# A hybrid decoder step: the four quadrant sums of each stationary unit on GpSimd, two of them a product earlier

## The chip, the cores and the metric

The kernel runs on one core of one Trainium2 chip. A core has TensorE (PE in the profile; its weight loads are PEld), VectorE (DVE), ScalarE (ACT), GpSimd (POOL) and SyncE (SP), which here only starts transfers, and 16 DMA engines. The time is the device time of one execution in microseconds. The kernel before takes 2857.4 us, the median of three runs (2855.56 to 2859.32). What is compared is the median of the changed kernel's runs with that of the kernel before.

## The reference

One inference step of one decoder layer for a prompt of 2048 rows and for 8 sample requests of 4 rows each, with shared weights, d = 1024, everything in fp32. Cut to what matters:

```python
m, s_gla, s_ssm, conv_buf = mixer(rmsnorm(x, lw['ln_mix_pre']), ...)   # two recurrent head groups
h = x + rmsnorm(m, lw['ln_mix_post'])                                  # m ends in  mixed @ w_out
a = cross_attend(rmsnorm(h, lw['ln_xa_pre']), mk, mv, w_xq, w_xo)      # softmax over 256 memory rows, 4 heads
h = h + rmsnorm(a, lw['ln_xa_post'])
hf = rmsnorm(h, lw['ln_ffn_pre'])
f = (jax.nn.silu(hf @ lw['w_gate']) * (hf @ lw['w_up'])) @ lw['w_down']  # d_ff = 2816
h = h + rmsnorm(f, lw['ln_ffn_post'])
```

The outputs are both hidden states, the recurrent states, the convolution's last rows and the memory's keys and values. The change touches the second part of the kernel, from `w_out` to `w_down`, which in the profiled execution begins at about 862 us and lasts to the end.

## The kernel before, in words

The first part makes the mixer's projections and its recurrence, chunk by chunk. The second part is a chain of nine passes over the prompt: `o` (`w_out`), `s` (attention scores), `v` (attention values), three blocks `g` of gate and up (over row groups 0 to 2, 3 to 5, and 6 to 7 with 16 sample columns beside them), and three parts `d` of the down projection. All of them are matrix products in fp32 that TensorE makes from pairs: each operand x is split into a rounded high part and a remainder, x = hi + lo, and a product is three matmuls, hi·hi, hi·lo and lo·hi (`three`, L134 to L136).

**Units and products.** Each pass multiplies many stationary *units* by seven moving *pieces*. A unit is a 2x2 arrangement of quadrants q0 to q3, and a block product is made from seven products in place of eight (a Strassen-Winograd scheme), taken in the order `TURN = [0, 1, 3, 2, 5, 4, 6]`. Three of the seven use q0, q1 and q3 themselves. The other four use sums of quadrants: S1 = q2 + q3 (product 3), S2 = S1 - q0 (product 2), S4 = q1 - S2 (product 5), S3 = q0 - q2 (product 4). S2 needs S1, and S4 needs S2. There are 114 units: 8 in each of `o`, `s`, `v`, 22 in each block `g` (11 column groups, gate then up) and 8 in each part `d`. So there are 456 sums, each 128 partitions by 512 columns (384 in the 8 units of the first part `d`).

**How one unit is prepared.** The class `Unit` (L1545 to L1578) loads the raw unit into a tile `raw` (two buffers, a transfer started by SyncE). `op` (L1554 to L1558) makes one sum into a tile `sum`, which has two buffers, so that the third and fourth sum of a unit reuse those of the first and second. `hi(i)` makes what product i needs: the sum, if there is one, then the high part into a tile `s` (four buffers) with a ScalarE copy (L1576), and it returns the VectorE instruction that makes the remainder (L1578), which is issued one product later. `part(e)` asks for this four products ahead of the product that TensorE is on (`ahead_ = 4`); it first issues the remainder of the entry before, then calls `hi` for its own.

**The moving side.** The class `Pieces` (L1609 to L1670) does the same for the pieces: ScalarE L1645 for the high part, VectorE L1649 for the remainder, from a staging tile `st` into tiles `r` (and `e`). This work is heavy where a pass begins. In the first and last unit of a pass it stands between the unit's own steps.

**Evacuation.** A unit's products go to three accumulators in PSUM (`accA`, two buffers, `accB` and `accC`, one each). `quads` (L1740) takes them out in `o`, `s` and `v` (ScalarE L1752, VectorE L1754), `evac_gate` (L1870) and `evac_up` (L1885) in the blocks `g`. There VectorE adds (L1902), multiplies by the gate (L1903) and in the third block the sample columns too (L1905), and a GpSimd transfer writes the result (L1909). `evac_d` does it for the parts `d`.

**What sets the order.** The order of each engine is the order in which the program issues: `pin` ties every instruction to the one issued before it on its engine. Per product the program issues the matmuls, the evacuation, `part` for the entry four ahead, a step of the moving side, then a step of the work that runs behind (`posts`, `aux`, `back`). An engine does not pass over an instruction that waits.

**GpSimd** has in this part the transfers to DRAM (`hX`, `out_y`, `xq`, `pT`, `xp`, `wT`, `aT`, `yp`), the one-column reciprocal roots of the norms (L142), and in the first block `g` some work of the samples (L1142).

Of the kernel before, what the change touches and what calls it, by code (L numbers as in the profile page):

```python
# [16 lines left out]
ALU = mybir.AluOpType  # L17
# [20 lines left out]
def f(ap):  # L38
    return ap.bitcast(F32)
# [3 lines left out]
def hymba_kernel(ctx: ExitStack, tc: tile.TileContext, a: dict, o: dict, dbg: dict | None = None):  # L43
    nc = tc.nc
# [75 lines left out]
    def wload(src, pieces=1, pool=None, raws=None):  # L120
        raw = (raws or wp).tile([P, 1024], F32, name="wraw", bufs=2)
        nc.sync.dma_start(out=raw, in_=src)
        hi, lo = ((pool or wp).tile([P, 1024], F32R, name=n, bufs=1 if pool else 3) for n in ("whi", "wlo"))
        w = 1024 // pieces
        with tc.high_priority(offset=AHEAD):
            for c in range(pieces):
                cs = slice(c * w, (c + 1) * w)
                last[0] = nc.scalar.activation(hi[:, cs], raw[:, cs], AF.Copy)  # L128
                nc.vector.tensor_tensor(lo[:, cs], raw[:, cs], f(hi)[:, cs], op=ALU.subtract)  # L129
        return raw, hi, lo  # L130
# [1414 lines left out]
    class Unit:  # L1545
# [8 lines left out]
        def op(self, out, x, y, o):  # L1554
            t, q = self.t, self.q
            t[out] = pf.tile([P, 512], F32, name="sum", bufs=2)[:, 0:self.w].rearrange("p (k c) -> p k c", c=P)
            x, y = (q[i] if isinstance(i, int) else t[i] for i in (x, y))
            nc.vector.tensor_tensor(t[out], x, y, op=o)  # L1558

        def hi(self, i):  # L1560

            if i == 1:
                self.op("S1", 2, 3, ALU.add)
            if i == 3:
                self.op("S2", "S1", 0, ALU.subtract)
            if i == 2:
                self.op("S4", 1, "S2", ALU.subtract)
            if i == 5:
                self.op("S3", 0, 2, ALU.subtract)
            v = {0: self.q[0], 1: self.q[1], 6: self.q[3]}  # L1570
            v = v[i] if i in v else self.t[{3: "S1", 2: "S2", 5: "S4", 4: "S3"}[i]]
            w = self.w
            s = pf.tile([P, 1024], F32R, name="s", bufs=4)
            hi, lo = s[:, 0:w], s[:, 512:512 + w]
            h3, l3 = (x.rearrange("p (k c) -> p k c", c=P) for x in (hi, lo))
            nc.scalar.activation(h3, v, AF.Copy)  # L1576
            self.got[i] = hi, lo
            return lambda: nc.vector.tensor_tensor(l3, v, f(h3), op=ALU.subtract)  # L1578
# [735 lines left out]
```

## Time and profile before

| | |
|---|---|
| median of the runs | 2857.4 us (2855.56, 2857.4, 2859.32) |
| the profiled execution's own time | 2854.98 us |
| its span | 2853.3 us |
| mean granted TensorE clock | 0.99 |
| TensorE, matmuls (PE) | busy 2757.0 us, 97% of the span |
| TensorE, weight loads (PEld) | 2362.4 us, beside the matmuls |
| VectorE (DVE) | 2074.9 us, 73%, 3820 instructions |
| ScalarE (ACT) | 1486.6 us, 52%, 2926 instructions |
| GpSimd (POOL) | 526.2 us, 18%, 716 instructions |
| the sums (L1558 on VectorE) | 228 + 114 + 114 instructions, median 0.68 to 0.69 us each |
| the remainders (L1578 on VectorE) | 456 from sums, 342 from raw quadrants, mean 0.68 us |
| the high parts (L1576 on ScalarE) | 456 from sums, 342 from raw quadrants, mean 0.62 us |

Busy time counts the running of instructions, not their waits, and starting a transfer is not busy time. A row of instructions in the profile reads: line, engine, operation, tile written, tiles read, shapes. Then come the count, the busy time with the mean of one in ns, and the idle time of the engine ahead of these instructions with what ended it. A row of the timeline reads: start in us, duration in us, engine, line, operation, and in brackets the idle time ahead and what ended it.

### The profile page before, as it was taken

Reading aid. Unit: us, or ns where it says so; the run is one execution under the profiler, and the core shown is the slowest. Engines: PE = TensorE matmul, PEld = TensorE weight load, DVE = VectorE, ACT = ScalarE, POOL = GpSimd, SP = SyncE. Lnnn points to the kernel's source line nnn. Section 1 sums busy time; section 2 is a strip of 40 time slices with the busy share of each in tenths; the row PEclk is TensorE's granted clock in tenths of the full one; section 3 lists DMA queues with packets and bytes.
Section 4 is the critical chain, followed back from the end, with each engine's and each line's share of the span. In section 5 each row is a group of like instructions: output and inputs, shape, how many; then the busy total and the mean of one; then the engine's idle time right before and its main releaser. Section 6 shows DMA issues by size and latency. Waiting matters only on the chain. (4 is left out here: it accounts for less than half of the span.)

```text
span 2853.3 us, 41834 instructions
## 1 busy us (share of the span) xinstructions
PE 2757.0 (97%) x15207; PEld 2362.4 (83%) x15207; DVE 2074.9 (73%) x3820; ACT 1486.6 (52%) x2926; POOL 526.2 (18%) x716
## 2 busy tenths in 40 slices
PE   8999999999997999999899999999999999999998
PEld 8887887787875878878798888889999998778786
DVE  7677777766747787677787787768678888564676
ACT  5545554544545777777754534434445555353432
POOL 2132342331321321015321110001000000000011
PEclk9999999999999999999999999999999999999999
DMA  7345535342256886468855566774234436574865
GB/s 252 115 135 181 153 106 163 111 146 88 79 180 227 295 278 223 148 188 254 275 200 187 186 222 233 263 251 165 97 130 176 150 122 208 185 213 102 244 150 131
DMA packets 151871, 514.27 MB, mean 180 GB/s; under 512 B 18336, under 2 KB 29776, under 8 KB 138096
## 3 DMA queue, kind: packets, MB, share of 16 engines
q1 hardware_dynamic: 95712, 336.01, 36.0%
q0 software_dynamic: 43712, 150.60, 16.6%
q10 hardware_dynamic: 12240, 24.99, 2.7%
q8 instruction: 120, 1.97, 0.3%
q14 instruction: 87, 0.71, 0.1%
HBM read 365.76 MB, written 145.76 MB: 179 GB/s over the span
## 5 line engine op out<-in xcount | busy, mean ns | idle before, releaser
L134 PE MATMUL accA<-r,s 128*128 128x512 f32 (+2 forms) x1792 | 641.8, 358 | 27.4 <-ACT r L1645 7.9
L136 PE MATMUL accA<-r,s 128*128 128x512 f32 (+2 forms) x1792 | 631.1, 352 | 1.7 <-DVE s L1578 1.6
L135 PE MATMUL accA<-r,s 128*128 128x384 f32 (+2 forms) x1472 | 504.8, 343 | 1.9 <-DVE r L1649 1.9
L134 PEld LDWEIGHTS accA<-r,s 128*128 128x128 f32 x1792 | 340.6, 190 | 86.3 <-issue 17.7
L1576 ACT ACTIVATE s<-sum 128x512 fp32r<-128x512 f32 (+1 forms) x456 | 282.3, 620 | 217.1 <-DVE sum L1558 92.1
L136 PEld LDWEIGHTS accA<-r,s 128*128 128x128 f32 x1792 | 340.2, 190 | 34.2 <-DVE s L1578 2.8
L134 PE MATMUL accC<-r,s 128*128 128x512 f32 (+2 forms) x896 | 318.6, 356 | 9.2 <-ACT s L1576 3.8
L1578 DVE TENSOR_TENSOR s<-sum,s 128x512 fp32r<-128x512 f32 (+1 forms) x456 | 305.6, 677 | 21.6 <-ACT s L1576 21.2
L136 PE MATMUL accC<-r,s 128*128 128x512 f32 (+2 forms) x896 | 314.2, 351 | 0.2
L135 PEld LDWEIGHTS accA<-r,s 128*128 128x128 f32 x1472 | 280.2, 190 | 21.3 <-DVE r L1649 5.0
L1578 DVE TENSOR_TENSOR s<-raw,s 128x512 fp32r<-128x512 f32 (+1 forms) x342 | 232.3, 679 | 52.5 <-ACT s L1576 50.7
L1576 ACT ACTIVATE s<-raw 128x512 fp32r<-128x512 f32 (+1 forms) x342 | 213.3, 624 | 72.0 <-PE accC L136 53.8
L135 PE MATMUL accC<-r,s 128*128 128x384 f32 (+2 forms) x736 | 250.5, 340 | 0.3 <-DVE r L1649 0.3
L128 ACT ACTIVATE whi<-wraw 128x1024 fp32r<-128x1024 f32 (+2 forms) x148 | 137.1, 940 | 187.6 <-PE acc L135 98.1
L129 DVE TENSOR_TENSOR wlo<-wraw,whi 128x1024 fp32r<-128x1024 f32 (+2 forms) x148 | 167.2, 1139 | 64.0 <-ACT whi L128 63.3
L134 PEld LDWEIGHTS accC<-r,s 128*128 128x128 f32 x896 | 168.9, 189 | 37.4 <-ACT sg L1877 5.3
L136 PEld LDWEIGHTS accC<-r,s 128*128 128x128 f32 x896 | 169.1, 189 | 16.2 <-DVE s L1578 0.9
L142 POOL TENSOR_TENSOR rs<-ms,nhalf 128x1 f32<-128x1 f32 (+4 forms) x125 | 113.4, 908 | 373.5 <-DVE ms L140 357.3
L134 PE MATMUL acc<-xh,whi 128*128 128x512 f32 (+1 forms) x464 | 168.5, 364 | 8.4 <-ACT xh L289 8.3
L136 PE MATMUL acc<-xh,wlo 128*128 128x512 f32 (+1 forms) x464 | 164.5, 356 | 1.7 <-DVE wlo L129 1.7
L135 PE MATMUL acc<-xl,whi 128*128 128x512 f32 (+1 forms) x464 | 164.1, 355 | 0.2 <-DVE xl L290 0.2
L134 PE MATMUL accB<-r,s 128*128 128x512 f32 (+2 forms) x448 | 157.6, 352 | 0.0
(644 smaller groups left out, 5847.9 us busy)
## 6 DMA issues: line engine op xcount, KB each, us to landing
raw<-in_w_gu_dram SPq DMA_DIRECT2D x66, 1024.0 KB, 4.9
wraw<-in_w_in_fm_dram SPq DMA_DIRECT2D x52, 512.0 KB, 3.7
wraw<-in_w_in_tm_dram SPq DMA_DIRECT2D x48, 512.0 KB, 3.7
st<-in_w_down_dram SPq DMA_DIRECT2D x37, 512.0 KB, 6.5
aT<-og POOLq DMA_DIRECT2D x22, 768.0 KB, 4.2
yp<-y POOLq DMA_DIRECT2D x32, 512.0 KB, 6.7
raw<-aT SPq DMA_DIRECT2D x16, 1024.0 KB, 6.4
out_y_dram<-y POOLq DMA_DIRECT2D x28, 512.0 KB, 6.0
```

What stands on the lines that cost most here:

```text
L128: last[0] = nc.scalar.activation(hi[:, cs], raw[:, cs], AF.Copy)
L129: nc.vector.tensor_tensor(lo[:, cs], raw[:, cs], f(hi)[:, cs], op=ALU.subtract)
L134: nc.tensor.matmul(ps, lhsT=wh, rhs=ah, start=start, stop=False, skip_group_check=more)
L135: nc.tensor.matmul(ps, lhsT=wh, rhs=al, start=False, stop=False, skip_group_check=more)
L136: nc.tensor.matmul(ps, lhsT=wl, rhs=ah, start=False, stop=stop, skip_group_check=more)
L142: nc.gpsimd.tensor_tensor(out=rs[:rows, :cols], in0=ms[:rows, :cols], in1=nhalf[:rows, :cols], op=ALU.pow)
L1576: nc.scalar.activation(h3, v, AF.Copy)
L1578: return lambda: nc.vector.tensor_tensor(l3, v, f(h3), op=ALU.subtract)
```

## The change

The four sums are made by GpSimd instead of VectorE. S1 is asked for together with product 0 of the unit instead of product 1, and S2 together with product 1 instead of product 3, each one entry of `TURN` earlier. S4 (with product 2) and S3 (with product 5) keep their places. What is computed, the tiles and their numbers of buffers are the same.

```diff
@@ -1555,13 +1555,13 @@
             t, q = self.t, self.q
             t[out] = pf.tile([P, 512], F32, name="sum", bufs=2)[:, 0:self.w].rearrange("p (k c) -> p k c", c=P)
             x, y = (q[i] if isinstance(i, int) else t[i] for i in (x, y))
-            nc.vector.tensor_tensor(t[out], x, y, op=o)
+            nc.gpsimd.tensor_tensor(out=t[out], in0=x, in1=y, op=o)
 
         def hi(self, i):
 
+            if i == 0:
+                self.op("S1", 2, 3, ALU.add)
             if i == 1:
-                self.op("S1", 2, 3, ALU.add)
-            if i == 3:
                 self.op("S2", "S1", 0, ALU.subtract)
             if i == 2:
                 self.op("S4", 1, "S2", ALU.subtract)
```

VectorE in the third block `g` (256 rows and 16 sample columns), around the evacuation of an up unit; `s` is the pair of a unit's operand, `sum` a sum, `t` and `og` the evacuation's tiles. Before:

```order
L1903 TENSOR_TENSOR og<-t,sg 128x2x128
L1905 TENSOR_TENSOR s_f<-t,sg 128x16
L1578 TENSOR_TENSOR s<-raw,s 128x512
L1558 TENSOR_TENSOR sum<-raw 128x512
L1902 TENSOR_TENSOR t<-accA,t 128x272
L1903 TENSOR_TENSOR og<-t,sg 128x2x128
L1905 TENSOR_TENSOR s_f<-t,sg 128x16
L1578 TENSOR_TENSOR s<-raw,s 128x512
L1558 TENSOR_TENSOR sum<-sum,raw 128x512
L1578 TENSOR_TENSOR s<-sum,s 128x512
L1558 TENSOR_TENSOR sum<-raw,sum 128x512
L1903 TENSOR_TENSOR og<-accA,sg 128x2x128
```

and now:

```order
L1903 TENSOR_TENSOR og<-t,sg 128x2x128
L1905 TENSOR_TENSOR s_f<-t,sg 128x16
L1578 TENSOR_TENSOR s<-raw,s 128x512
L1902 TENSOR_TENSOR t<-accA,t 128x272
L1903 TENSOR_TENSOR og<-t,sg 128x2x128
L1905 TENSOR_TENSOR s_f<-t,sg 128x16
L1578 TENSOR_TENSOR s<-raw,s 128x512
L1578 TENSOR_TENSOR s<-sum,s 128x512
L1903 TENSOR_TENSOR og<-accA,sg 128x2x128
```

The three sums are gone from VectorE's row; the rest stands in the order it had. Two remainders, which were apart by a sum, now follow each other.

GpSimd in the values pass `v`, where `y` is an evacuated row group, `u` and `st` what is written for the blocks `g`, and `rs` a reciprocal root. Before:

```order
L1852 DMA xp<-st 128x512 x2
L142 TENSOR_TENSOR rs<-ms,nhalf 128x1
L1725 DMA y<-hX 128x1024
L1852 DMA xp<-u 128x512 x2
L1796 DMA out_y_dram<-y 128x1024
L142 TENSOR_TENSOR rs<-ms,nhalf 128x1 x2
L1725 DMA y<-hX 128x1024
L1852 DMA xp<-u 128x512 x2
L1796 DMA out_y_dram<-y 128x1024
```

and now:

```order
L1852 DMA xp<-st 128x512 x2
L142 TENSOR_TENSOR rs<-ms,nhalf 128x1
L1725 DMA y<-hX 128x1024
L1852 DMA xp<-u 128x512 x2
L1558 TENSOR_TENSOR sum<-raw 128x512
L1796 DMA out_y_dram<-y 128x1024
L142 TENSOR_TENSOR rs<-ms,nhalf 128x1 x2
L1725 DMA y<-hX 128x1024
L1558 TENSOR_TENSOR sum<-sum,raw 128x512
L1852 DMA xp<-u 128x512 x2
L1558 TENSOR_TENSOR sum<-raw,sum 128x512
L1796 DMA out_y_dram<-y 128x1024
```

Three sums have come between GpSimd's transfers and roots: S1 ahead of the first output transfer, S2 and S4 around the two transfers of `xp`. The transfers and roots keep their order among themselves.

## The prediction

> **What bounds the kernel now.** I read the share of each engine first, then the engines' busy time in stretches cut at the points where a pass begins, then what TensorE waited for.
>
> ```profile
> PE 2757.0 (97%) x15207; PEld 2362.4 (83%) x15207; DVE 2074.9 (73%) x3820; ACT 1486.6 (52%) x2926; POOL 526.2 (18%) x716
> ...
> 862.00:912.00 50.00, 38.12 (x130) 26.26 (x131) 35.94 (x46) 29.07 (x47) 2.58 (x3) 0.88 0.59 207
> 1384.00:1420.00 36.00, 24.05 (x112) 20.69 (x111) 27.00 (x46) 25.46 (x55) 13.00 (x19) 0.85 0.83 274
> 1784.00:2134.00 350.00, 346.98 (x2091) 325.50 (x2090) 250.99 (x427) 157.26 (x294) 24.76 (x41) 1.00 0.52 181
> 2154.00:2384.00 230.00, 227.86 (x1768) 220.29 (x1768) 188.92 (x373) 123.96 (x253) 7.14 (x10) 1.00 0.42 147
> 2384.00:2398.00 14.00, 9.27 (x50) 7.58 (x49) 12.08 (x24) 6.17 (x12) 0.71 (x1) 0.76 0.73 251
> sum 1982.00, PE 1921.57 PEld 1670.00 DVE 1479.09 ACT 1060.73 POOL 279.09; mean PE 147.81 PEld 128.46 DVE 113.78 ACT 81.59 POOL 21.47
> ```
>
> The columns of a stretch are its length, then PE, PEld, DVE, ACT and POOL busy, the granted clock and the DMA load. The last row sums all stretches from 862 to 2844, where the units run. TensorE is busy 1921.6 of 1982.0 us, so it idles 60.4 us in all. Of that, 11.9 + 12.0 + 4.7 us lie in three short stretches in which a pass begins; inside a pass it idles 3.0 of 350 and 2.1 of 230 us. VectorE is busy 1479.1 (75%). Nothing that relieves VectorE can bring more than these 60.4 us and what the clock loses beside them. What ended TensorE's waits:
>
> ```profile
> PE accA L134 <- ACT r L1645: 7.9, 7, 3.8
> PE accA L135 <- DVE e L1649: 7.0, 8, 1.6
> PE accA L134 <- DVE y L1754: 5.8, 1, 5.8
> PE accA L134 <- DVE t L1902: 5.0, 2, 4.7
> ...
> PE accC L134 <- ACT s L1576: 3.8, 1, 3.8
> PE accA L134 <- ACT s L1576: 3.6, 2, 3.0
> ...
> PE accA L136 <- DVE s L1578: 1.6, 2, 1.3
> ```
>
> The pieces of the moving side (L1645, L1649) and two evacuations lead. The pairs that the four sums feed (s, L1576 and L1578) ended 9.0 us of waits in five places.
>
> **What it removes.** 456 sums leave VectorE; those of the block with most pressure are
>
> ```profile
> L1578 DVE TENSOR_TENSOR s<-sum,s 128x512 fp32r<-128x512 f32 x83 | 55.9, 684 | 4.2 <-ACT s L1576 4.2
> L1578 DVE TENSOR_TENSOR s<-raw,s 128x512 fp32r<-128x512 f32 x60 | 41.2, 686 | 4.6 <-ACT s L1576 3.8
> L1558 DVE TENSOR_TENSOR sum<-raw 128x512 f32<-128x512 f32 x41 | 28.2, 688 | 0.7
> L1558 DVE TENSOR_TENSOR sum<-raw,sum 128x512 f32<-128x512 f32 x21 | 14.5, 692 | 0.7
> L1558 DVE TENSOR_TENSOR sum<-sum,raw 128x512 f32<-128x512 f32 x21 | 14.4, 684 | 0.0
> L1903 DVE TENSOR_TENSOR og<-t,sg 128x256 f32<-128x256 f32 x31 | 13.2, 426 | 1.1
> ```
>
> which is VectorE from 2154 to 2384. At 0.69 us each, 456 sums are about 313 us, 21% of VectorE's work in the stage. By itself this is worth almost nothing, because the engine that waits is TensorE and it hardly waits for VectorE.
>
> **What it adds.** 456 two-operand sums on GpSimd. The trace has three like them, 128x512 in fp32:
>
> ```profile
> L778 POOL TENSOR_TENSOR xD<-xD,y x16: 1300/1592/1669, 153.4 to 785.6; 128x512 f32<-128x512 f32 x16
> L781 POOL TENSOR_TENSOR z<-xD,z x16: 1287/1296/1313, 158.8 to 789.0; 128x512 f32<-128x512 f32 x16
> L743 POOL TENSOR_TENSOR xw<-xdt,wl__6835 x4: 1038/1046/1047, 728.9 to 777.7; 128x512 f32<-128x512 f32 x4
> ```
>
> The three numbers are minimum, median and maximum in ns. L743 reads one operand as a broadcast of few columns; the sums read two dense ones like L781, so I take 1.30 us, with 1.04 and 1.67 as ends. 456 x 1.30 = 593 us on an engine that has 279 us in this stage: 872 of 1982 us, 44%. GpSimd has the room. The Trainium skill (GPSIMD Engine Reference, section 4.1, Engine selection) puts elementwise work on VectorE because GpSimd is about twice as slow with two inputs; 1.30 against 0.69 us is that ratio, so the trace agrees. Its 4497 ns for 2048 elements gives an estimate of 1.12 us, and 513 us for the 456.
>
> The price that counts is another. A GpSimd sum holds up a VectorE instruction that reads two operands from SBUF:
>
> ```profile
> 2202.70 1.28 DVE L1578 TENSOR_TENSOR s<-sum,s 128x512 fp32r<-128x512 f32 x2
> ...
> 370.90 2.36 DVE L765 TENSOR_TENSOR M<-M,cbm 128x512 f32<-128x512 f32 x2
> 371.06 1.65 POOL L778 TENSOR_TENSOR xD<-xD,y 128x512 f32<-128x512 f32 x1 [2.88 <-DVE y L777]
> ...
> 1547.39 1.03 POOL L1142 TENSOR_TENSOR Ms<-Ms,sell 128x512 f32<-128x512 f32 x1 [1.60 <-DMA Ms<-in_state_ssm_dram]
> 1547.46 1.51 DVE L1578 TENSOR_TENSOR s<-sum,s 128x512 fp32r<-128x512 f32 x1
> ```
>
> Two such instructions alone take 1.28 us; with one GpSimd instruction between them they take 2.36, so it costs VectorE 1.08 us. At 1547 the very instruction that follows our sums, the remainder L1578, takes 1.51 instead of 0.68 and ends 0.55 us after GpSimd does. The Trainium skill says why (Advanced Engine Details and Errata, GPSIMD Details): GpSimd shares a read and a write interface with VectorE and conflicts with two-SBUF-input instructions. These rows agree.
>
> So the sums do not leave that path; each takes 1.08 us (or up to 1.30, the whole instruction) of it instead of 0.64. In the tightest block, 2154 to 2384, the path carries 143 remainders at 0.64 (91.5), 13.2 of L1903 and 83 sums at 1.08 (89.6): 194 of 230 us, 84%; at 1.30 it is 213 us, 92%. It fits, barely. In the other blocks of gate and up the same work stands against a longer time: by 350 us for 22 units, where this one has some 21 in 230, it is below 65%.
>
> **What it moves.** S1 and S2 are asked for one product earlier. In the tightest block they stand in VectorE's densest run, and ScalarE waits for them:
>
> ```profile
> 2206.41 0.44 DVE L1902 TENSOR_TENSOR t<-accC,t 128x272 f32<-128x272 f32 x1 [1.45 <-PE accC L136]
> ...
> 2207.91 0.69 DVE L1558 TENSOR_TENSOR sum<-raw 128x512 f32<-128x512 f32 x1
> ...
> 2208.72 0.63 ACT L1576 ACTIVATE s<-sum 128x512 fp32r<-128x512 f32 x1 [1.75 <-DVE sum L1558]
> ...
> 2212.14 0.63 ACT L1576 ACTIVATE s<-sum 128x512 fp32r<-128x512 f32 x1 [0.71 <-DVE sum L1558]
> ...
> 2215.45 0.39 PE L134 MATMUL accC<-r,s 128*128 128x272 f32 x1
> ```
>
> With the new position S1 and S2 depend only on the raw tile and on buffers that are free by then, so they fall into the 1.45 us of rest before 2206.41 and the time before it. The third sum, S4, keeps its position; ScalarE splits it at 2212.14, after 0.71 us of waiting, and TensorE first uses it at 2215.45, 2.7 us after that split ends. Even 1.30 us plus one hold of 1.08 stays inside this. So: no stall from late sums, value 0, bounds 0 and the case below.
>
> S4 and S3 now also wait on GpSimd for remainders that VectorE makes of S1 and S2 (their two buffers are reused), and behind them stand GpSimd's own DMAs. The longest such delay is in the values pass:
>
> ```profile
> 1303.25 0.83 POOL L1796 DMA_DIRECT2D out_y_dram<-y  x1
> ...
> 1306.41 0.69 DVE L1578 TENSOR_TENSOR s<-sum,s 128x512 fp32r<-128x512 f32 x1 [0.17 <-ACT s L1576]
> ...
> 1316.46 0.59 ACT L1752 COPY y<-accC 128x512 f32<-128x512 f32 x1
> ...
> out_y_dram<-y POOLq DMA_DIRECT2D x28, 512.0 KB, 6.0
> ```
>
> S4 waits for the remainder that ends at 1307.10 and takes 1.30; the output DMA behind it goes at about 1308.4 instead of 1303.25, lands 6.0 us later at 1314.4, and the copy that reuses its buffer runs at 1316.46. Hidden, with 2 us to spare. Elsewhere a DMA or a reciprocal root behind one sum is late by one sum, 1.3 us, against a product of 2.0 us (twelve matmuls; 2091 of them in 350 us), 1.6 in the tightest block (1768 in 230).
>
> **The sum.** (1) The first unit: S1 and S2 leave a dense run of VectorE for the rest that stands ahead of it.
>
> ```profile
> 863.25 1.23 DVE L1649 TENSOR_TENSOR r<-st,r 128x1024 fp32r<-128x1024 f32 x1 [2.95 <-ACT r L1645]
> ...
> 866.46 0.69 DVE L1558 TENSOR_TENSOR sum<-raw 128x512 f32<-128x512 f32 x1
> ```
>
> 2 x 0.64 = -1.3; ends: that, and +1.1, one hold. (2) The eight other beginnings of a pass: a sum less (-0.6) or a hold more (+1.1) each, -4.8 to +8.8; no row says which, and I take the nearer to nothing, +0.5 in all. (3) The tightest block: at 84 to 92% of the shared path an occasional hold reaches TensorE; 0 to +28 (below), I take +1.0. Together +0.2 us: 2855.0 becomes 2855.2 in the profiled execution's terms, which stand 2.4 below the median of the runs; against that median I say 2857.6, rounded to **2858**, no change. What a measurement can tell from none here is about 0.2%, 5.7 us.
>
> **Rivals.**
>
> A, slower: from 2154 to 2384 the shared path becomes the bound. VectorE works in order, so its instructions on PSUM operands (L1881, L1902, and the rest of its 188.9 us) cannot slip past a held remainder. The sum of everything: 188.9 less 57.1 for the sums is 131.8; with 83 x 1.08 it is 221, with 83 x 1.30 it is 240, and if instructions that overlap by 0.08 now no longer do, some 143 x 0.08 = 11 more: 251. It decides from 230 on; 0 to +21, and up to +28 with the 1.67 of L778 in a third of the sums. I price it at +13: 2870. For it speaks 92%; against it that PSUM work runs beside GpSimd (L1902 and its like are not lengthened) and that S1 and S2 come early.
>
> B, faster: the chain of waits gives the sums a share,
>
> ```profile
> by line: PE accA L134 6.5%; PE accA L135 6.3%; PE accA L136 6.3%; PE accC L134 3.6%; PE accC L136 3.4%; PE accC L135 3.4%; PE accB L134 1.7%; PE accB L136 1.6%; PE accB L135 1.6%; issue 1.3%; DVE s L1578 0.8%; DVE sum L1558 0.7%; DMA st<-xp
> ```
>
> 0.7% of 2853.3 is 20 us. If half of it is gained, with a slow stretch of the clock or two less, the time is 2846. Against it: TensorE hardly idles where the chain runs through the sums.
>
> C, slower by GpSimd's queue: the output DMAs of the values pass land late (the spare is 2 us) and the buffer's next copy waits; 2 us in each of seven units is +14: 2872.
>
> **Numbers.** Forecast 0.48 (its own range 2852 to 2863), A 0.26, B 0.20, C 0.06. Faster by more than 0.2%: B's 0.19 and 0.03 of the forecast's tail, 0.22; slower: A's 0.22, C's 0.05 and 0.03 of the tail, 0.30; within: the rest, 0.48. The range that is to hold it 8 times in 10 cuts half of B and the upper part of A, 0.1 each: 2847 to 2873.
>
> **What would show it.** Right: TensorE's idle time from 862 to 2844 stays near 60 us; L1558 on GpSimd at 1.3 to 1.6 us; the mean of L1578 rises from 0.68 to 0.9 or more; VectorE's busy time falls by much less than 313 us; ScalarE's waits for sums shrink for S1 and S2. A shows as TensorE's idle time between 2154 and 2384, ended by s (L1576 or L1578). B shows as shorter waits at 862 to 912 and 1384 to 1420. C shows as ScalarE's copy to y waiting for the output DMA. I am wrong if GpSimd takes much more than 1.3 us, or several sums in a row hold VectorE.

## The result and the profile after

The changed kernel takes 2871.9 us, the median of four runs (2871.0 to 2875.9), against 2856.5 for the kernel before (four runs, 2854.9 to 2859.3). The ratio is 1.006, with a 95% interval of 1.0048 to 1.0072. So the change makes the kernel 15 us slower, where no change was forecast. Times of the experiments below are compared with the kernel before on the same chip, which took 2852.9 to 2855.3 us there. A ratio is formed from all runs and a difference from the medians, so the two need not agree to the last digit.

The first part of the page of the changed kernel, with the share of each engine:

```profile
PE 2762.1 (96%) x15207; PEld 2373.2 (83%) x15207; DVE 2008.8 (70%) x3364; ACT 1487.6 (52%) x2926; POOL 1166.3 (41%) x1172
```

VectorE lost 456 instructions of together 313 us, but its busy time fell by 66.1 us only (2074.9 to 2008.8). So the other instructions became 247 us longer together, 0.54 us for each sum; I call such a lengthening of a VectorE instruction by a running GpSimd instruction a hold. TensorE's busy time rose by 5.1 us, though it has the same 15207 matmuls.

Where the time went shows when stretches are cut at the same work. The changed kernel's stretches, with the columns of the prediction's first fence (length, PE, PEld, VectorE, ScalarE, GpSimd, clock, DMA load, GB/s):

```profile
1384.00:1420.00 36.00, 24.72 (x117) 21.55 (x116) 28.14 (x42) 26.46 (x57) 20.30 (x24) 0.88 0.87 276
1420.00:1800.00 380.00, 361.79 (x2133) 330.77 (x2132) 289.86 (x513) 177.44 (x334) 171.61 (x170) 0.97 0.57 199
1800.00:2150.00 350.00, 347.19 (x2086) 324.68 (x2085) 221.08 (x338) 155.98 (x293) 148.91 (x129) 1.00 0.52 179
2150.00:2170.00 20.00, 14.28 (x90) 13.05 (x89) 16.35 (x23) 9.56 (x21) 6.32 (x6) 0.90 0.58 201
2170.00:2400.00 230.00, 228.26 (x1781) 222.77 (x1781) 188.92 (x293) 125.94 (x255) 124.50 (x93) 0.99 0.44 153
```

The same work of the first gate/up block in the kernel before, and one short stretch in it:

```profile
1420.00:1784.00 364.00, 357.42 (x2139) 323.96 (x2138) 295.56 (x597) 177.84 (x335) 54.34 (x85) 1.00 0.60 208
...
1455.00:1475.00 20.00, 18.91 (x108) 18.34 (x107) 19.77 (x61) 8.81 (x17) 0.69 (x2) 1.00 0.49 158
```

The first gate/up block takes 380 us for what took 364: the whole loss is there. Of the 16.0 us, 11.6 are idle time of TensorE (18.2 against 6.6) and 4.4 are matmuls that take longer; the granted clock is 0.97 there. In the third block, where the prediction saw the danger, TensorE does 1781 matmuls in 230 us where it did 1768, though in the 20 us ahead of it, where the pass begins, it is busy 14.3 us where it was busy 16.5. That is the block with most pressure from the sums, but the first one is the block in which the samples' work runs behind the prompt's: there VectorE is busy 19.77 of 20 us in the stretch at 1455 already before the change.

What TensorE waited for from 1420 to 1800 in the changed kernel (us in total, times, longest):

```profile
PE accA L134 <- DVE sg L1881: 3.9, 2, 2.8
PE mx L1039 <- DVE sdA L1034: 3.3, 1, 3.3
PE mx L1124 <- DVE ssq L1121: 3.1, 1, 3.1
PE mx L1215 <- DVE sBm L1212: 2.9, 4, 1.4
PE mx L1278 <- DVE s_x L1307: 2.7, 1, 2.7
```

and in the same block before:

```profile
PE mx L1140 <- DVE sBm L1137: 3.2, 2, 1.6
PE accA L134 <- DVE sg L1881: 1.1, 2, 0.8
PE mx L1278 <- DVE s_x L1307: 0.6, 1, 0.6
PE mx L1124 <- DVE ssq L1121: 0.3, 1, 0.3
...
PE mx L1039 <- DVE sdA L1034: 0.3, 1, 0.3
```

Four single waits have grown to 2.7 to 3.3 us, from 0.3 to 0.8. (The waits for `sBm` have shifted: at L1215 2.7 us more, at L1140 1.8 less.) Three of the four end at a matmul of the samples (L1039, L1124, L1278) that stands in TensorE's order between the prompt's matmuls, and at a VectorE result. The fourth, `sg`, ends at 1458.88 behind VectorE's preparation for the samples (L964 to L988 and L1012 to L1019); no sum runs on GpSimd in the 6 us ahead of its end, so this one isn't explained by a sum that holds something. None of the four ends at a sum or at a unit's pair `s`. The timeline shows what delays the first of these results, `sdA`, in the changed kernel. It is the end of the samples' softplus, a chain of products (L167) and additions (L168) of 32x8 elements:

```profile
1493.59 1.29 POOL L1558 TENSOR_TENSOR sum<-raw 128x512 f32<-128x512 f32 x1 [1.50 <-DVE spe L163]
1493.73 1.16 DVE L167 TENSOR_TENSOR spp<-spp,spe 32x8 f32<-32x8 f32 x1
...
1495.12 0.15 DVE L167 TENSOR_TENSOR spp<-spp,spe 32x8 f32<-32x8 f32 x1
...
1497.47 1.75 POOL L1558 TENSOR_TENSOR sum<-raw 128x512 f32<-128x512 f32 x1 [2.59 <-DVE spp L168]
1497.99 1.24 DVE L167 TENSOR_TENSOR spp<-spp,spe 32x8 f32<-32x8 f32 x1
...
1499.29 1.26 POOL L1558 TENSOR_TENSOR sum<-sum,raw 128x512 f32<-128x512 f32 x1
1499.46 1.11 DVE L167 TENSOR_TENSOR spp<-spp,spe 32x8 f32<-32x8 f32 x1
...
1502.08 0.15 DVE L1034 TENSOR_TENSOR sdA<-sdt,ahead 32x8 f32<-32x8 f32 x1
...
1502.28 0.23 PE L1039 MATMUL mx<-sdA,bm 32*32 32x8 f32 x2 [3.28 <-DVE sdA L1034]
```

In the kernel before the chain begins at 1491.99 and TensorE goes on at 1497.48 after a wait of 0.25 us:

```profile
1491.99 0.15 DVE L167 TENSOR_TENSOR spp<-spp,spe 32x8 f32<-32x8 f32 x1
...
1497.27 0.15 DVE L1034 TENSOR_TENSOR sdA<-sdt,ahead 32x8 f32<-32x8 f32 x1
...
1497.48 0.22 PE L1039 MATMUL mx<-sdA,bm 32*32 32x8 f32 x2 [0.25 <-DVE sdA L1034]
```

A product of 0.15 us takes 1.11 to 1.24 us when a GpSimd sum runs. Three such holds are 3.1 us, and the chain from the first product to `sdA` takes 8.35 us instead of 5.28. TensorE waits those 3.1 us and pays again behind the wait:

```profile
1500.00:1504.00 4.00, 1.72 (x14) 1.20 (x15) 2.67 (x12) 1.42 (x4) 0.55 (x1) 0.96 0.00 0
1504.00:1512.00 8.00, 8.00 (x29) 6.25 (x30) 3.63 (x11) 1.44 (x3) 0.00 (x0) 0.59 0.17 37
```

These are two stretches of the changed kernel. In the second, the granted clock is 0.59 and TensorE does 29 matmuls in 8 us; before, it does 62 in the 10 us from 1500. The Trainium skill (TensorE: Matmul & The Clock Gate, Part 1) gives half the clock after an idle window of about 3.4 us; here waits of 2.7 to 3.3 us were followed by it. Over the 4 to 8 us behind each of the four waits (1459 to 1463, 1504 to 1512, 1565 to 1569, 1725 to 1733) the granted clock is 0.57 to 0.59. So on these traces a shorter wait can do it. Where the bound lies isn't shown: a wait of 1.8 us has 0.57 behind it in one of the runs below (first block undone), and one of 1.9 us has 1.00 in another (five units at the waits).

The waits for `ssq` and `s_x` come from holds too, the second only in part. Ahead of `ssq` a remainder takes 2.05 us instead of 0.68 and L1119, a product of 128x128, 1.78 instead of 0.29, each beside a sum. Ahead of `s_x` a sum holds L1229 (1.24 us instead of 0.14), and the next sum stands ahead of a reciprocal root in GpSimd's own queue:

```profile
1717.75 1.24 DVE L1229 TENSOR_TENSOR st<-s_sq 32x1 f32<-32x1 f32 x1
...
1719.02 0.14 DVE L140 TENSOR_SCALAR ms<-st 32x1 f32<-32x1 f32 x1
1719.06 1.29 POOL L1558 TENSOR_TENSOR sum<-sum,raw 128x512 f32<-128x512 f32 x1
...
1720.30 1.02 POOL L142 TENSOR_TENSOR rs<-ms,nhalf 32x1 f32<-32x1 f32 x1
```

The root L142 starts 1.14 us after the value that it needs; in the kernel before it starts 0.08 us after it (1707.15 against 1707.07). So of the 2.1 us by which this wait grew, about half is the hold and half GpSimd's queue.

### The profile page after: what moved, and what is told of

Its sections match the earlier page's. It is cut to its first block, busy times and chain, and to the rows that moved or that the text cites. A ratio compares the mean times of both kernels' runs of the same rounds, so it can differ in the third digit from the quotient of the medians.

```text
span 2869.3 us, 42324 instructions
## 1 busy us (share of the span) xinstructions
PE 2762.1 (96%) x15207; PEld 2373.2 (83%) x15207; DVE 2008.8 (70%) x3364; ACT 1487.6 (52%) x2926; POOL 1166.3 (41%) x1172
## 3 DMA queue, kind: packets, MB, share of 16 engines
q0 software_dynamic: 43712, 150.60, 16.5%
## 5 line engine op out<-in xcount | busy, mean ns | idle before, releaser
L1578 DVE TENSOR_TENSOR s<-sum,s 128x512 fp32r<-128x512 f32 (+1 forms) x456 | 375.3, 830 | 57.3 <-ACT s L1576 56.0
L1558 POOL TENSOR_TENSOR sum<-raw 128x512 f32<-128x512 f32 (+1 forms) x228 | 316.2, 1387 | 185.3 <-DVE s L1578 124.4
L1558 POOL TENSOR_TENSOR sum<-raw,sum 128x512 f32<-128x512 f32 (+1 forms) x114 | 157.2, 1379 | 440.7 <-DVE s L1578 392.0
L1578 DVE TENSOR_TENSOR s<-raw,s 128x512 fp32r<-128x512 f32 (+1 forms) x342 | 283.1, 828 | 33.8 <-ACT s L1576 33.7
L1558 POOL TENSOR_TENSOR sum<-sum,raw 128x512 f32<-128x512 f32 (+1 forms) x114 | 176.6, 1549 | 42.1 <-DVE s L1578 35.2
L142 POOL TENSOR_TENSOR rs<-ms,nhalf 128x1 f32<-128x1 f32 (+4 forms) x125 | 113.7, 911 | 166.3 <-DVE ms L140 164.3
```

What stands on the lines that cost most here:

```text
L142: nc.gpsimd.tensor_tensor(out=rs[:rows, :cols], in0=ms[:rows, :cols], in1=nhalf[:rows, :cols], op=ALU.pow)
L1558: nc.gpsimd.tensor_tensor(out=t[out], in0=x, in1=y, op=o)
```

## The experiments

The theory after this reading, **H**: in the first gate/up block a running GpSimd sum holds the samples' small VectorE instructions, TensorE's sample matmuls wait, and the clock falls behind the wait. The rivals were the moved positions (P), the prediction's rival A (the third block is full), a small loss in every pass (S), late sums or a late GpSimd queue (D), and the samples' matmuls, which stand at some places of TensorE's order a few matmuls earlier or later since the change (R).

**The engine alone, and the places alone.** The first keeps the old positions of S1 and S2 and uses GpSimd; the second moves them and stays on VectorE.

```diff
-            if i == 0:
+            if i == 1:
                 self.op("S1", 2, 3, ALU.add)
-            if i == 1:
+            if i == 3:
                 self.op("S2", "S1", 0, ALU.subtract)
```

```diff
-            nc.gpsimd.tensor_tensor(out=t[out], in0=x, in1=y, op=o)
+            nc.vector.tensor_tensor(out=t[out], in0=x, in1=y, op=o)
```

> The four sums on GpSimd, but S1 and S2 asked for where they were before. Theory H (in the first gate/up block, 1420 to 1784 us before, a GpSimd sum holds the samples' small VectorE instructions, TensorE's sample matmuls wait for them and the clock dips behind each such wait): the number of sums is the same, so the loss stays, +11 to +18 us, 2868 to 2875. Rival P (the earlier places do it, because the sums now run beside the samples' work and no longer between the remainders): below +5, 2856 to 2861. Rival A of the prediction (the third gate/up block is full): +11 to +18 too, but TensorE's idle time between 2154 and 2400 us grows by 8 or more.

> The two earlier places alone, all sums on VectorE. H: nothing is held, -3 to +3 us, 2853 to 2860. Rival P: +10 or more, 2866 and above.

The engine alone takes 2879.0 us against 2852.9: +26 us, ratio 1.0083 (1.0068 to 1.0098), more than any theory expected. The places alone take 2849.3: -3.6 us, ratio 0.9986 (0.9976 to 0.9995). So P falls, and the earlier places are worth something: 3.6 us on VectorE, and more on GpSimd, where a sum takes longer and is waited for longer. By the medians it is 10.6 us there (26.1 less 15.5), by the ratios (1.0083 against 1.0060) less than 7; these are two separate comparisons whose intervals just touch. ScalarE's waits for the sums show it, in the list of those who waited for a sum: with the places alone

```profile
  ACT s L1576: 48.7, 40
```

where the kernel before has 112.4 us in 87 waits, the changed kernel 93.6 in 82, and the engine alone 133.7 in 103.

**The first block undone, and the first block alone.** One kernel has the change except in the 22 units of the first gate/up block; the other has it only there.

```diff
-            nc.gpsimd.tensor_tensor(out=t[out], in0=x, in1=y, op=o)
+            (nc.gpsimd if self.k != XG else nc.vector).tensor_tensor(out=t[out], in0=x, in1=y, op=o)
...
+            pool = self.k != XG
-            if i == 0:
+            if i == (0 if pool else 1):
                 self.op("S1", 2, 3, ALU.add)
-            if i == 1:
+            if i == (1 if pool else 3):
                 self.op("S2", "S1", 0, ALU.subtract)
```

Here `k` is the number of the unit's pass and `XG` that of the first block; the reverse has `==` for `!=`.

> As the change, but in the 22 units of the first gate/up block the sums stand as before, on VectorE and in the old places. H: of the 15 us lost some 13 come back; -1 to +4 us against the kernel before, 2856 to 2861, and TensorE's waits for sdA, ssq and s_x are back under 0.7 us each. Rival A, and rival S (every pass loses a little from held remainders): +10 us or more, 2866 and above.

> The reverse: only the 22 units of the first gate/up block have the change, 88 of the 456 sums. H: +11 to +16 us, 2868 to 2873, nearly the whole loss from a fifth of the sums. Rival A or S: 0 to +4, below 2861.

Without the first block the time is 2855.0, ratio 1.0003 (0.9993 to 1.0012): nothing clear of noise is left of the loss, with 368 sums on GpSimd. With the first block alone it is 2870.6, +17.7 us, ratio 1.0056 (1.0041 to 1.0071): the whole loss from 88 sums. A and S fall.

**Idle sums and idle copies.** The kernel before, with VectorE making all sums. Beside each sum of the first block (from the time the block's tiles exist) GpSimd makes something that nobody reads. TensorE's order is that of the kernel before, row for row, so neither a late sum nor another order (R) can act; GpSimd's own queue can still be late.

```diff
             nc.vector.tensor_tensor(t[out], x, y, op=o)
+            if self.k == XG and pg:
+                idle = pg.tile([P, 512], F32, name="idle", bufs=1).rearrange("p (k c) -> p k c", c=P)
+                nc.gpsimd.tensor_tensor(out=idle, in0=q[2], in1=q[3], op=ALU.add)
```

The copies have `nc.gpsimd.tensor_copy(out=idle, in_=q[2])` as the last line.

> The kernel before, VectorE making all sums in the old places, TensorE's order unchanged row for row; beside each sum of the first gate/up block GpSimd also adds two quadrants into a tile that nobody reads. Nothing depends on GpSimd here. H (the hold by itself costs the time): +8 to +18 us, 2861 to 2871 by the time of 2853 that the kernel before has on this chip, with the waits for sdA, ssq or s_x again 2 us and longer. Rival D (the sums come late from GpSimd, or its queue is late) and rival R (the sample matmuls stand at other places in TensorE's order since the change): -2 to +3 us.

> As the run with the idle sums, but GpSimd copies one quadrant into the unread tile: one operand in place of two. If any GpSimd instruction on SBUF holds VectorE for its length, +5 to +18 us by that length; if only two-operand ones do, -2 to +3 us.

With idle sums the time is 2908.7, +55 us, ratio 1.0197 (1.018 to 1.0214); with idle copies 2860.7, +7 us, ratio 1.0027 (1.0017 to 1.0036). So late sums and R aren't needed for a loss: work on GpSimd that nobody waits for costs three times what the change costs. VectorE here has its own sums and the holds as well, and is busy 370 us of the block's 420. The size was far outside what I expected. The copies hold too, at 0.82 us each instead of 1.46, so a GpSimd instruction with one operand holds as well.

**Idle sums in the third block.** The same edit with `self.k == XG + 2`.

> The kernel before, with the idle GpSimd sums beside VectorE's own in the third gate/up block, the one that rival A of the prediction names; TensorE's order is unchanged. VectorE has 188.9 of 230 us there; some 83 idle sums at the 0.59 us of hold that the change shows in this block make 238, at the 1.08 of the prediction 279. If the hold is 0.59: +5 to +15 us. If it is 1.08: +35 to +50. If VectorE's fullness doesn't bind there: 0 to +3.

It takes 2897.4, +42 us, ratio 1.0151 (1.0136 to 1.0167), which is in the range expected for a hold of 1.08. VectorE has the same order as before, row for row, so each VectorE instruction can be set beside its counterpart. The stretch of the block in this run:

```profile
2154.00:2430.00 276.00, 242.40 (x1793) 226.16 (x1794) 271.80 (x381) 126.34 (x259) 130.10 (x90) 1.00 0.36 127
```

and VectorE's costliest groups in it, the remainders (L1581 here) and the first of the sums:

```profile
L1581 DVE TENSOR_TENSOR s<-sum,s 128x512 fp32r<-128x512 f32 x84 | 84.7, 1026 | 0.0
L1581 DVE TENSOR_TENSOR s<-raw,s 128x512 fp32r<-128x512 f32 x62 | 62.8, 1012 | 0.0
L1558 DVE TENSOR_TENSOR sum<-raw 128x512 f32<-128x512 f32 x42 | 44.9, 1068 | 0.7
```

VectorE is busy 271.8 of 276 us: it is the bound, and a remainder takes 1.03 us instead of 0.68. Set side by side over this stretch, 92 of the 297 instructions with all operands in SBUF overlap an idle sum and are together 83 us longer; of 82 with an operand in PSUM, 28 overlap one and none is longer. So the 80 idle sums of the stretch cost 83 us, 1.04 us each. VectorE had 41 us free in the block (230 less 188.9), which leaves 42 us, and 42 were measured.

**Quarters.** The change in the first block alone, each sum in four instructions of 128 columns.

```diff
+                for c in range(4):
+                    nc.gpsimd.tensor_tensor(out=t[out][:, c], in0=x[:, c], in1=y[:, c], op=o)
```

> The change in the first gate/up block alone, each sum made by four GpSimd instructions of 128 columns. If a held instruction of VectorE waits until the one running GpSimd instruction ends, a small one then waits about 0.35 us and not 1.3: +2 to +8 us against the kernel before. If GpSimd's total time at the port decides: +11 to +17, as with whole sums.

2873.8, +20 us, ratio 1.0071 (1.0053 to 1.0089). The run doesn't separate what it was made for, because a quarter takes more than a quarter of 1.3 us: four in a row take 1.72 us. It does show both patterns:

```profile
1487.22 3.75 DVE L1583 TENSOR_TENSOR s<-raw,s 128x512 fp32r<-128x512 f32 x1 [0.20 <-ACT s L1581]
...
1497.22 1.72 POOL L1560 TENSOR_TENSOR sum<-raw 128x128 f32<-128x128 f32 x4 [0.78 <-DVE spe L163]
1497.37 0.33 DVE L167 TENSOR_TENSOR spp<-spp,spe 32x8 f32<-32x8 f32 x1
1497.73 0.39 DVE L168 TENSOR_SCALAR spp<-spp 32x8 f32<-32x8 f32 x1
```

Small instructions get in between the quarters at 0.33 to 0.39 us, but the remainder at 1487 lasts 3.75 us, while GpSimd makes eight quarters in a row. Shorter instructions are no remedy here.

**The chain's operand in PSUM.** The change in the first block alone, with the operand e of the samples' softplus in PSUM.

```diff
-        e = pl.tile([P, 32], F32, name="spe")[:rows, :w]
+        e = (mxt() if rows == NS else pl.tile([P, 32], F32, name="spe"))[:rows, :w]
```

> The change in the first gate/up block alone, and the operand e of the samples' softplus chain (L154 to L170) lies in PSUM, so that its products read one operand from SBUF and one from PSUM. TensorE's rows for it move five matmuls later, about 0.9 us. H: the products are not held, all stay at 0.15 to 0.2 us, TensorE's wait for sdA (3.3 us) is gone and the clock dip behind it: 3 to 8 us less than with the change in that block alone (2870.6), so 2863 to 2868. If PSUM operands do not escape the hold: within 2 us of 2870.6.

2869.8 against 2870.6 with the change in that block (ratios 1.0057 and 1.0056, each against its own kernel before): no difference. The expectation fell, though the products did escape:

```profile
1493.15 1.29 POOL L1558 TENSOR_TENSOR sum<-raw 128x512 f32<-128x512 f32 x1 [1.18 <-DVE mx L163]
1493.31 0.15 DVE L167 TENSOR_TENSOR spp<-spp,mx 32x8 f32<-32x8 f32 x1
1493.49 0.97 DVE L168 TENSOR_SCALAR spp<-spp 32x8 f32<-32x8 f32 x1
...
1496.45 1.75 POOL L1558 TENSOR_TENSOR sum<-raw 128x512 f32<-128x512 f32 x1 [2.01 <-DVE spp L168]
1496.98 0.14 DVE L167 TENSOR_TENSOR spp<-spp,mx 32x8 f32<-32x8 f32 x1
1497.16 1.07 DVE L168 TENSOR_SCALAR spp<-spp 32x8 f32<-32x8 f32 x1
```

All seven products take 0.14 to 0.15 us, and the addition behind them, with its one operand in SBUF, pays the hold instead. TensorE's wait for `sdA` is still 2.4 us. So the hold isn't a matter of two operands alone, as the prediction had it. The Trainium skill (SBUF — State Buffer, SBUF: two separate sides) has the pair of ports held for the whole instruction and the other engine blocked, by instructions with two SBUF inputs or in a 2-port mode. The rows agree with the block for a whole instruction; no run here shows which mode L168 runs in. Nor is every instruction with one operand in SBUF held. In the changed kernel a step of a norm, L140 on 128x1, takes its 0.15 us in the midst of a sum:

```profile
1052.28 1.30 POOL L1558 TENSOR_TENSOR sum<-raw,sum 128x512 f32<-128x512 f32 x1 [5.35 <-DVE sq L1729]
1052.45 0.15 DVE L140 TENSOR_SCALAR ms<-sq 128x1 f32<-128x1 f32 x1
```

**Five units at the waits, and five others.** The change in the first block alone, less five of its 22 units.

```diff
+            pool = self.k == XG and self.n not in (27, 29, 30, 33, 42)
```

Here `n` is the unit's number in the whole order, 24 being the first of the block. The other five are 25, 31, 36, 38 and 44.

> The change in the first gate/up block alone, but for five of its 22 units (the 4th, 6th, 7th, 10th and 19th), whose sums are made in the stretches in which TensorE then waits for sg, sdA, ssq and s_x; these five stand as in the kernel before. Theory L (the loss is local: a held chain of the samples at four places, and the clock behind it): 10 us or more of the 18 come back, below 2861 where the kernel before has 2853. Theory T (VectorE's total over the block decides): 5/22 of it come back, 4 us, 2866 or so.

> The same with five other units (the 2nd, 8th, 13th, 15th and 21st), whose sums lie away from those waits. L: 0 to 4 us come back, 2866 to 2871. T: 4 us, 2866.

With the five units at the waits the time is 2859.3, +4.0 us, ratio 1.0018 (1.0007 to 1.0029): 14 of the 18 us come back. With five others it is 2872.8, +17.5 us, ratio 1.0061 (1.0045 to 1.0077): nothing comes back. So the loss is local. The stretch around `sdA`, first in the changed kernel, with TensorE's 3.3 us wait:

```profile
1493.00:1513.00 20.00, 16.72 (x83) 14.14 (x82) 14.02 (x41) 8.13 (x15) 4.30 (x3) 0.83 0.20 70
```

and then with the five units back on VectorE:

```profile
1493.00:1513.00 20.00, 19.75 (x121) 18.03 (x120) 17.77 (x55) 10.66 (x21) 0.76 (x1) 1.00 0.23 85
```

121 matmuls instead of 83 in the same 20 us, at full clock. TensorE's waits for `s_x`, `ssq` and `sdA` in that run are those of the kernel before, but the one for `sg` is not:

```profile
PE accA L134 <- DVE sg L1882: 4.6, 2, 4.4
...
PE mx L1124 <- DVE ssq L1121: 0.3, 1, 0.3
PE mx L1039 <- DVE sdA L1034: 0.3, 1, 0.3
```

So what came back belongs to three of the four waits. The wait for `sg` is 4.4 us here though the sums made around it are on VectorE again, and 3.2 us with the places alone, where GpSimd makes no sum at all. What sets it is not shown, and neither is whether it is what is left of the loss here.

**A version that beats both.** The places alone is one (2849.3, above). Its trace loses some 3.5 us in the first block, where TensorE waits 3.2 us for `sg` until 1456.42, so the last run keeps the old places there.

```diff
+            early = self.k != XG
-            if i == 0:
+            if i == (0 if early else 1):
                 self.op("S1", 2, 3, ALU.add)
-            if i == 1:
+            if i == (1 if early else 3):
                 self.op("S2", "S1", 0, ALU.subtract)
```

> All sums on VectorE, S1 and S2 in the earlier places except in the 22 units of the first gate/up block, which stand as before. With the earlier places everywhere the trace is 3.8 us ahead of the kernel before at 1411 us, loses 3.5 of it at 1468, where TensorE waits 3.2 us for sg, and ends 6 ahead. If that loss comes from the earlier places in this block: -5 to -9 us against the kernel before. If the earlier places gain there too on balance: -2 to -4, no better than with them everywhere (-3.6).

2849.1 against 2853.8, -4.7 us, ratio 0.9989 (0.998 to 0.9998). It is faster than the kernel before, and not to be told from the places everywhere, whose interval is 0.9976 to 0.9995. What the earlier places do in the first block stays open. Where they gain is the third block: with the places alone

```profile
2150.60:2380.60 230.00, 228.88 (x1787) 222.32 (x1785) 190.70 (x376) 125.26 (x257) 7.14 (x10) 1.00 0.42 150
```

it is 1787 matmuls in 230 us and 1788 in the last run, where the kernel before does 1768 and three runs that have the third block as before (the first block alone, and twice less five units) do 1765 or 1766 of the same work. At 0.13 us each, 19 more are 2.5 us of the 3.6. The engine alone does 1788 there as well, so either half of the change gains in this block.

## Why the prediction was wrong

**What bounds the kernel: right.** The end is set by TensorE. Its idle time after 862 us rose from 60.4 to 72.3 us (1998.0 less 1925.8, from 862 to 2860), its busy time by 4.2; together this is the 16.0 us by which the span grew.

**The cost of a sum on GpSimd: right in kind.** Forecast 1.30 us (1.04 to 1.67); measured 1.43 in the mean over the second part.

**The hold: right in kind, mis-sized, and too narrow.** The prediction put 1.08 us of VectorE's time for each sum in place of 0.64. In the changed kernel it is 0.54 in the mean, less than the sum itself; that fits sums that fall where VectorE has nothing to be held, which wasn't counted. At 1.04 us it was near the forecast where VectorE has no gap (idle sums in the third block). It also holds some instructions with one operand in SBUF. The forecast mean of 0.9 us or more for the remainder was high: 0.83.

**The step that failed** is this one: "In the other blocks of gate and up the same work stands against a longer time: by 350 us for 22 units, where this one has some 21 in 230, it is below 65%." It reads the first block as if it held the units' work alone. The samples' work runs in it too, and a cut into stretches shows it: VectorE busy 295.6 of 364 us (81%), and 19.8 of 20 us at 1455. So the sum has no term for this block, which cost 16 us. More than that, a share was the wrong measure. VectorE as a whole was relieved there by the change (295.6 to 289.9 us in a longer block). What counts is that at three places (`sdA`, `ssq`, `s_x`) TensorE waits for the end of a chain of VectorE instructions, and that a chain instruction of 0.15 us can pay most of a GpSimd sum. At `s_x` another sentence failed too: a root behind a sum "is late by one sum, 1.3 us, against a product of 2.0 us". It was 1.1 us late, and nothing hid it. The forecast of the third block, +1.0 us, came out as some 1.7 us gained (13 more matmuls in 230 us, at 0.13 us each), so the worry over the densest block was misplaced. Against it go the 2.2 us less that TensorE is busy where this pass begins, in the term of the eight other beginnings (+0.5 us).

**S1 and S2 earlier: valued at 0, measured at 3.6 us gained alone**, and more with the sums on GpSimd. Most of it is gained in the third block, where "no stall from late sums, value 0" stood; the price of what waits for S1 and S2 there wasn't worked out. The 1.3 us forecast for the first unit can't be read from the traces: its first matmul starts at 863.21 instead of 863.79, but in the traces of runs whose code up to there is that of the kernel before it starts anywhere from 861.35 to 864.75. The same holds for the beginnings of a pass up to the first gate/up block: at 1404 the change is 1.4 us ahead of the kernel before, and such runs lie between 4.3 us ahead and 0.3 behind.

**GpSimd's queue in the values pass: right.** The output transfer that I put at about 1308.4 goes at 1308.19, and no copy waits for it.

**The rivals.** A had the mechanism (a held path of VectorE becomes the bound) and the size, 2870 against 2871.9, but in the wrong block, and by a share instead of by a chain; that its number came out is luck. The range, 2847 to 2873, holds the time on A's account and not the forecast's. B and C don't appear. Slower by more than 0.2% had a chance of 0.30.

## What to carry to other kernels

When elementwise work goes from VectorE to GpSimd, it isn't VectorE's busy share that decides; look for chains of small VectorE instructions with operands in SBUF that an in-order TensorE waits for, and price each link at up to the whole length of one GpSimd instruction. Search every stretch in which a second stream of work runs beside the loop, not only the densest one, and add what a wait of some 3 us costs again in clock. If a producer can simply be asked for one step earlier, try that by itself first: here it was the only part of the change that shortened the whole kernel.

## What the runs showed of the hardware

A GpSimd instruction of 1.3 us lengthens a VectorE instruction of 0.15 us to 1.1 to 1.2 us. It does so when the VectorE instruction reads two operands from SBUF (92 cases with idle sums in the third block, 83 us) and not when an operand lies in PSUM (28 cases, none longer). Of those with one operand, all in SBUF, some are held (L168 on 32x8, 0.97 and 1.07 us) and some are not (L140 on 128x1, 0.15 us). The hold goes the other way as well: in the changed kernel a sum that begins at 1213.58 takes 3.86 us while VectorE runs three instructions with two SBUF operands one behind the other, at their usual 0.68 and 1.21 us. A copy on GpSimd, with one operand, holds too (82 copies of 0.82 us, +7 us). Taking the first victim out of the hold's way passed it on to the next instruction in SBUF. A sum cut into four took 1.72 us of GpSimd instead of 1.30. And half of TensorE's clock came after waits of 2.7 to 3.3 us.
